# A hybrid decoder layer: the 16 meta tokens worked in tiles of 128 partitions, with the high and low halves of their operands in one matmul

## The chip, the cores and the metric

One core of one Trainium2 chip runs the whole layer as one program. The metric is device microseconds of one execution; a measurement is the median of several runs. "Full clock" below is TensorE's granted clock of 2.4 GHz, "half clock" 1.2 GHz.

## The reference

The layer puts 16 learned meta tokens ahead of 1024 tokens of width 1024, normalises the stream and projects it once. Two mixers share the projection: retention with 4 heads of 128, worked in chunks of 128 tokens of which the meta tokens are a partial first one, and sparse attention with 8 heads of 64, where an indexer picks the top 256 keys of each query. Output projection and a squared-ReLU MLP follow, and the meta tokens are dropped.

```python
h = jnp.concatenate([meta, x], axis=1)
u = rmsnorm(h, norm1_w[l]).astype(h.dtype)
proj = u @ w_in[l]
...
y_ret = retention(rq, rk, rv, rg, ret_norm_w[l], pos)
y_dsa = sparse_attention(dq, dk, dv, iq, ik, iw, q_norm_w[l], k_norm_w[l], rel_bias, pos, topk)
h = h + jnp.concatenate([y_ret, y_dsa], axis=-1) @ w_out[l]
u = rmsnorm(h, norm2_w[l])
h = h + jnp.square(jax.nn.relu(u @ w_ff1[l])) @ w_ff2[l]
return h[:, N_META:]
```

## The kernel before, in words

Matmuls run in a reduced-precision form of float32 (fp32r). To keep accuracy, an operand is split into a high half (a ScalarE copy to fp32r) and a low half (what is left, a VectorE or GpSimd subtract), and a product becomes three matmuls: high by high, low by high, high by low. Tokens are worked in eight blocks of 128; the meta tokens are a ninth block, b == 8, of 16 partitions.

`proj` (L225 to L231) projects one block: for each of 8 slices of the width, three matmuls with the block's inputs as weights (128 or, for the meta block, 16 columns) and a slice of the weight matrix streaming past. `umh` and `uml` hold the meta block's inputs. `small_proj` (L254) gives the index key, attention key and value of a block; for values, `vv[:, b]` holds the high half in 64 columns and the low half in the next 64. `ret_meta` (L427) starts a retention head: it projects the meta tokens to keys and values, rotates the keys, and multiplies them by the values over 16 rows (L435) to the state `S`.

The program has these stages: normalisation and index scores (to about 190 us), retention of 4 heads by 8 chunks together with the top-k search on VectorE and ScalarE (to about 436 us), attention together with the output projection (to about 645 us), second normalisation, MLP. Attention goes by units, (block i, half of the heads g), i from 0 to 7. `attend_p` makes the scores and exponentials of a unit; `attend_v` (L571) multiplies its probabilities by the values. For each tile of keys, the meta tile first and then i + 1 tiles of 128, it transposes the probabilities of four heads on TensorE (L581), splits them (L587 on ScalarE, L588 on VectorE) into `ph` and `pl`, and adds `vv` by `ph` (L589) and `vv` by `pl` (L590) in PSUM. For the meta tile these have 16 rows.

Memory comes from pools. `p1` (called `big`) holds the working tiles of the index and retention stages and is closed by `stage.close()` (L768); then `p2` opens over the same memory, and the first writer of each of its tiles waits for the last readers of `p1`. The last of those is the store of a retention head's output (`oh`, scaled on VectorE in L485) to DRAM (L486). Python code is recorded in the order written; a list scheduler then orders each engine's instructions by its own estimate, and every engine executes its list strictly in that order. Waits between engines are semaphores.

Of the kernel before, what the change touches and what calls it, by code (L numbers as in the profile page):

```python
# [9 lines left out]
F32 = mybir.dt.float32  # L10
F32R = mybir.dt.float32r
# [9 lines left out]
NM = 16  # L21
NB = 8
# [58 lines left out]
def layer(ctx, tc, x, meta, norm1_w, w_in, ret_w, q_w, k_w, rel, w_out, norm2_w, w1, w2,  # L81
# [91 lines left out]
    umh = const.tile([128, 8, NM], F32R, name="umh")  # L173
    uml = const.tile([128, 8, NM], F32R, name="uml")

# [42 lines left out]
    def u_sl(b, d):  # L218
        if b == 8:
            return umh[:, d, :], uml[:, d, :]  # L220
        o = 128 * (b % 4)
        return uth[b // 4][d // 4][:, d % 4, o:o + 128], utl[b // 4][d // 4][:, d % 4, o:o + 128]

    def proj(ps, b, hs, ls, c0, n):
        P = NM if b == 8 else 128  # L225
# [7 lines left out]
    def do_norm1(b):  # L233
        if b == 8:
            xm = row("xt")
            nc.sync.dma_start(xm[:NM, :D], meta)
            norm_T(xm[:NM, :D], NM, lambda g: (umh[:, 4 * g:4 * g + 4, :], uml[:, 4 * g:4 * g + 4, :]))
# [9 lines left out]
    absw = const.tile([128, NB, 8], F32, name="absw")  # L247
    sgnw = const.tile([128, NB, 8], F32, name="sgnw")
    w8 = const.tile([128, NB, 8], F32, name="w8")
# [3 lines left out]
    def small_proj(b, hs, ls):  # L253
        P = NM if b == 8 else 128  # L254
        ps = psA()
        proj(ps, b, hs, ls, 0, NS)
        s = big.tile([128, NS], F32, name="smp", tag="fg", bufs=2)
        nc.scalar.activation(s[:P], ps[:P, :NS], AF.Copy)
# [4 lines left out]
        nc.vector.tensor_tensor(vv[:P, b, 64:128], s[:P, 136:200], vv[:P, b, 0:64].bitcast(F32), op=ALU.subtract)  # L263
        if b < 8:
# [120 lines left out]
    kgain = const.tile([128, 64], F32, name="kgain")  # L385
    nc.sync.dma_start(kgain, bcast(k_w, 64))
    qgain = const.tile([128, 64], F32, name="qgain")
# [26 lines left out]
    def rotate(ps, P, b, nqk, name):  # L414
# [5 lines left out]
        ro = big.tile([128, 2, 2, 64], F32, name="ro", tag="ro", bufs=2)  # L420
        nc.gpsimd.tensor_tensor(ro[:P, :nqk, 0], t1[:P, :nqk, 0], t2[:P, :nqk, 1], op=ALU.subtract)
# [5 lines left out]
    def ret_meta(h):  # L427
        hs, ls = st["w", h]
        ps = psA()
# [141 lines left out]
    def attend_v(i, g):  # L571
# [6 lines left out]
        for k, (b, k0, kp) in enumerate(tiles):  # L578
# [568 lines left out]
```

## Time and profile before

| | us |
|---|---|
| median of 3 runs | 1327.14 (1326.75 to 1327.76) |
| the profiled execution's own time | 1329.52 |
| its span, first to last instruction | 1327.7 |
| TensorE busy | 1271.8 (96%) |
| VectorE busy | 1076.9 (81%) |
| ScalarE busy | 750.4 (57%) |
| GpSimd busy | 260.8 (20%) |

PE is TensorE, PEld its weight loads, DVE VectorE, ACT ScalarE, POOL GpSimd, SP the engine that issues the transfers. Matmuls are pipelined, so the printed duration of one is longer than the time after which the next one starts. A matmul's form is printed as rows*columns of its weights, then the columns that stream past: 16*128 16x512 has 16 rows in use, 128 columns of weights and streams 512. A line number is that of the kernel before.

### The profile page before, as it was taken

The page shows a single profiled execution, that of the slowest core. Times are in us where ns is not written, and L with a number is a line of the kernel's source. Part 1 is how long each engine was busy: PE and PEld are TensorE (multiplying, and loading weights), DVE is VectorE, ACT ScalarE, POOL GpSimd, SP SyncE. Part 2 cuts the span into 40 slices and gives each one's busy share as a digit, 9 for nine tenths or more (in the row PEclk, how much of TensorE's full clock was granted, in tenths as well). Part 3 has the DMA queues.
Part 4 walks back from the last instruction along what each step waited for, and adds up shares of the span by engine and source line. Part 5 has one row for each costly group of instructions (what it writes and reads, how often), then busy time and mean ns, then how long its engine had stood idle before and what let it go on. Part 6 is the DMA issues. An engine that isn't in the chain of part 4 may idle for free. (4 is left out here: it accounts for less than half of the span.)

```text
span 1327.7 us, 18666 instructions
## 1 busy us (share of the span) xinstructions
PE 1271.8 (96%) x6200; PEld 1047.9 (79%) x6200; DVE 1076.9 (81%) x2387; ACT 750.4 (57%) x1593; POOL 260.8 (20%) x297
## 2 busy tenths in 40 slices
PE   6999999899899999999997999999999999999998
PEld 5888868687777778787775888888888888888887
DVE  5678999899979878676759877777878988887875
ACT  6676647577753667565756555555556444444442
POOL 4004472323434424220343000000000200000000
PEclk9999999899999899999998999999999999999999
DMA  9103040202201211212362434434538844434222
GB/s 283 57 17 90 33 133 9 72 11 71 64 16 49 95 64 49 67 45 72 112 213 88 156 130 161 148 129 173 175 135 298 334 160 159 158 134 184 96 95 96
DMA packets 93664, 153.74 MB, mean 116 GB/s; under 512 B 7240, under 2 KB 47344, under 8 KB 89856
## 3 DMA queue, kind: packets, MB, share of 16 engines
q1 hardware_dynamic: 93568, 152.56, 33.5%
q8 instruction: 49, 0.80, 0.2%
q14 instruction: 47, 0.39, 0.1%
HBM read 110.58 MB, written 43.46 MB: 116 GB/s over the span
## 5 line engine op out<-in xcount | busy, mean ns | idle before, releaser
L898 ACT ACTIVATE wh<-ga 128x512 fp32r<-128x512 f32 x144 | 87.2, 628 | 158.7 <-PE psB L1046 141.5
L229 PE MATMUL psA<-wh,uh 128*128 128x512 f32 x376 | 152.4, 406 | 4.4 <-DVE gs L455 4.3
L231 PE MATMUL psA<-wl,uh 128*128 128x512 f32 x376 | 150.4, 400 | 0.0
L230 PE MATMUL psA<-wh,ul 128*128 128x512 f32 x376 | 150.1, 399 | 0.0
L899 DVE TENSOR_TENSOR wl<-ga,wh 128x512 fp32r<-128x512 f32 x144 | 96.7, 687 | 47.4 <-ACT wh L898 46.8
L898 ACT ACTIVATE wh<-sum 128x512 fp32r<-128x512 f32 x128 | 78.6, 625 | 74.3 <-DVE sum L895 69.9
L1046 PE MATMUL psB<-wh,wl 128*128 128x512 f32 x280 | 108.9, 389 | 0.0
L1047 PE MATMUL psB<-wl,wh 128*128 128x512 f32 x280 | 108.9, 389 | 0.0
L1045 PE MATMUL psB<-wh 128*128 128x512 f32 x280 | 106.8, 389 | 0.0
L689 DVE TENSOR_SCALAR_CACHE_REDUCE jk_cnt<-sc,tcand 128x400 bf16<-128x400 f32 (+1 forms) x124 | 102.2, 824 | 1.0
L694 ACT ACTIVATE jk_top<-sc,tcand 128x272 bf16<-128x272 f32 (+2 forms) x93 | 85.0, 914 | 28.2 <-DVE tcand L728 23.6
L899 DVE TENSOR_TENSOR wl<-sum,wh 128x512 fp32r<-128x512 f32 x128 | 87.7, 685 | 6.4 <-ACT wh L898 4.7
L229 PEld LDWEIGHTS psA<-wh,uh 128*128 128x128 f32 x376 | 72.2, 192 | 19.0 <-issue 3.5
L191 POOL TENSOR_TENSOR wl<-wr,wh 128x512 fp32r<-128x512 f32 x56 | 80.9, 1460 | 31.2 <-PE psB L641 15.5
L965 POOL COPY ga<-wl 128x1 f32<-128x1 f32 x8 | 6.6, 826 | 401.6 <-PE psB L928 276.2
L231 PEld LDWEIGHTS psA<-wl,uh 128*128 128x128 f32 x376 | 71.9, 191 | 14.4
L230 PEld LDWEIGHTS psA<-wh,ul 128*128 128x128 f32 x376 | 72.4, 192 | 13.5
L587 ACT ACTIVATE ph<-psB 128x512 fp32r<-128x512 f32 (+1 forms) x88 | 51.3, 592 | 48.3 <-PE psB L581 40.3
L588 DVE TENSOR_TENSOR ph<-psB,ph 128x512 fp32r<-128x512 f32 (+1 forms) x88 | 59.4, 683 | 17.4 <-ACT ph L587 15.9
L335 ACT ACTIVATE rl<-psB,absw 128x320 f32<-128x320 f32 (+5 forms) x104 | 52.7, 554 | 36.4 <-PE psB L333 23.9
L1046 PE MATMUL psA<-wh,wl 128*128 128x512 f32 x168 | 65.4, 389 | 0.0
L1047 PE MATMUL psA<-wl,wh 128*128 128x512 f32 x168 | 65.4, 389 | 0.0
(354 smaller groups left out, 3669.9 us busy)
## 6 DMA issues: line engine op xcount, KB each, us to landing
ga<-hid SPq DMA_DIRECT2D x28, 1024.0 KB, 4.9
wr<-in_w_ff_dram SPq DMA_DIRECT2D x34, 512.0 KB, 4.8
hid<-hs SPq DMA_DIRECT2D x48, 256.0 KB, 2.0
wr<-in_w_in_dram SPq DMA_DIRECT2D x32, 256.0 KB, 3.2
gb<-in_w_ff_dram SPq DMA_DIRECT2D x8, 1024.0 KB, 4.9
ga<-in_w_ff_dram SPq DMA_DIRECT2D x8, 1024.0 KB, 5.6
wr<-in_w_out_dram SPq DMA_DIRECT2D x12, 512.0 KB, 3.8
xt<-in_x_dram SPq DMA_DIRECT2D x8, 512.0 KB, 4.6
```

What stands on the lines that cost most here:

```text
L191: (nc.vector if alt and altc[0] % 2 else nc.gpsimd).tensor_tensor(shl, raw, shp.bitcast(F32), op=ALU.subtract)
L229: nc.tensor.matmul(ps[:P, :n], uh, wh, start=d == 0, stop=False)
L230: nc.tensor.matmul(ps[:P, :n], ul, wh, start=False, stop=False)
L231: nc.tensor.matmul(ps[:P, :n], uh, wl, start=False, stop=d == 7)
L588: nc.vector.tensor_tensor(pl[:kp], tp[:kp], ph[:kp].bitcast(F32), op=ALU.subtract)
L689: nc.vector.tensor_scalar(jk_[:, :ncol[i]], sc[i], cand[:, j:j + 1], 0.0, op0=ALU.is_ge, op1=ALU.add, accum_out=cnt[:, j:j + 1])
L694: nc.scalar.activation(jk_top[:, :ncol[i]], sc[i], AF.Sign, scale=-1.0, bias=cand[:, j:j + 1], accum_out=cnt[:, j:j + 1])
L898: nc.scalar.activation(view(hi), s, AF.Copy)
L899: nc.vector.tensor_tensor(view(lo), s, view(hi).bitcast(F32), op=SUB)
L1045: nc.tensor.matmul(ps[tb], ah[:, t], bh, start=j == 0 and m not in CONT, stop=False, skip_group_check=True)
L1046: nc.tensor.matmul(ps[tb], al[:, t], bh, start=False, stop=False, skip_group_check=True)
L1047: nc.tensor.matmul(ps[tb], ah[:, t], bl, start=False, stop=j == NO - 1, skip_group_check=True)
```

## The change

Three things are done to the meta block. First, `um` replaces `umh` and `uml`: 48 columns of weights per slice, the high half in columns 0 to 15, zeros, the low half in 32 to 47. `proj_meta` streams the high half of the weight matrix past all 48 and its low half past the first 16, so 16 matmuls replace 24; the two results stand in different partitions of PSUM and are added (a ScalarE copy, then a VectorE add), for the small projection and for the four retention heads. Second, `vv[:, 8]` is zeroed and holds the values twice, in partitions 0 to 15 and 32 to 47, and a new tile `pm`, zeroed once, takes the high half of the meta probabilities in its first 16 partitions and the low half from partition 32 on: one matmul over 128 rows replaces two over 16. Third, the rotated key and the value tile of `ret_meta` are zeroed by GpSimd and multiplied over 128 rows. To make room, some small tables move between pools.

```diff
-    umh = const.tile([128, 8, NM], F32R, name="umh")
-    uml = const.tile([128, 8, NM], F32R, name="uml")
+    um = const.tile([128, 8, ML + NM], F32R, name="um")
+    nc.vector.memset(um.bitcast(F32), 0.0)
...
+    def proj_meta(hs, ls, c0, n, tag, bufs):
+
+        ps = psA()
+        for d in range(8):
+            if d:
+                nc.tensor.matmul(ps[:NM, :n], um[:, d - 1, :NM], ls[d - 1][:, c0:c0 + n], start=False, stop=False)
+            if d == 7:
+                nc.tensor.matmul(ps[:NM, :n], um[:, d, :NM], ls[d][:, c0:c0 + n], start=False, stop=False)
+            nc.tensor.matmul(ps[:ML + NM, :n], um[:, d, :], hs[d][:, c0:c0 + n], start=d == 0, stop=d == 7)
+        t, s = [big.tile([128, 256], F32, name="mt", tag=tag, bufs=bufs) for _ in range(2)]
+        nc.scalar.activation(t[:NM, :n], ps[ML:ML + NM, :n], AF.Copy)
+        nc.vector.tensor_tensor(s[:NM, :n], ps[:NM, :n], t[:NM, :n], op=ALU.add)
+        return s
...
+    nc.vector.memset(vv[:, 8].bitcast(F32), 0.0)
...
+        if b == 8:
+            s = proj_meta(hs, ls, 0, NS, "oh", 3)
...
+        if b == 8:
+            nc.scalar.activation(vv[ML:ML + NM, b], vv[:NM, b].bitcast(F32), AF.Copy)
...
+        if P < 128:
+            nc.gpsimd.memset(ro[:, :nqk], 0.0)
...
-        ps = psA()
-        proj(ps, 8, hs, ls, 128, 256)
-        km = rotate(ps, NM, 8, 1, "km")
+        kv = proj_meta(hs, ls, 128, 256, "qkT", 2)
+        km = rotate(kv, NM, 8, 1, "km")
         vm = big.tile([128, 128], F32, name="vm", tag="vz", bufs=2)
-        nc.scalar.activation(vm[:NM], ps[:NM, 128:256], AF.Copy, scale=vecs[:NM, 2, h:h + 1])
+        nc.gpsimd.memset(vm, 0.0)
+        nc.scalar.activation(vm[:NM], kv[:NM, 128:256], AF.Copy, scale=vecs[:NM, 2, h:h + 1])
         pd = psB()
-        nc.tensor.matmul(pd[:, 0:128], km[:NM, 0], vm[:NM], start=True, stop=True)
+        nc.tensor.matmul(pd[:, 0:128], km[:, 0], vm, start=True, stop=True)
...
+            if b == 8:
+                ph, pl = at["pm"], at["pm"][ML:]
             nc.scalar.activation(ph[:kp], tp[:kp], AF.Copy)
             nc.vector.tensor_tensor(pl[:kp], tp[:kp], ph[:kp].bitcast(F32), op=ALU.subtract)
-            nc.tensor.matmul(pv, vv[:kp, b, :], ph[:kp], start=k == 0, stop=False)
-            nc.tensor.matmul(pv, vv[:kp, b, :], pl[:kp], start=False, stop=k == len(tiles) - 1)
+            nc.tensor.matmul(pv, vv[:, b, :], ph, start=k == 0, stop=False)
+            if b < 8:
+                nc.tensor.matmul(pv, vv[:, b, :], pl, start=False, stop=k == len(tiles) - 1)
...
     stage.close()
     p2["p"] = ctx.enter_context(tc.tile_pool(name="p2", bufs=1))
+    at["pm"] = p2["p"].tile([128, 512], F32R, name="pm")
+    nc.vector.memset(at["pm"].bitcast(F32), 0.0)
```

The new line numbers are shifted: L485 becomes L506, L556 L577, L562 L583, L581 L602, L588 L611, L589 L612, L554 and L555 L575 and L576, L594 L618. The order of instructions moves in many places; two matter below. VectorE at the change of pools, before (the waits are named by the semaphore's engine; DMAHW are the transfers'):

```order
L556 ISA P,mn<-psA,mb 128x240 [waits PE_49]
L556 ISA mn 128x1
L485 SCALAR_TENSOR_TENSOR oh<-oh,rs_y,fg 128x128 [waits Pool_49]
L485 SCALAR_TENSOR_TENSOR oh<-oh,rs_y,fg 128x128 x3
L562 TENSOR_REDUCE m_5222<-mn 128x1 [waits DVE_49,Activation_49]
L562 TENSOR_REDUCE m_5245<-mn 128x1 [waits DVE_49,Activation_49]
L588 TENSOR_TENSOR ph<-psB,ph 128x512 [waits Activation_49]
```

The same place now:

```order
L506 SCALAR_TENSOR_TENSOR oh<-oh,rs_y,fg 128x128 [waits Pool_49]
L506 SCALAR_TENSOR_TENSOR oh<-oh,rs_y,fg 128x128 x3
L795 MEMSET pm 128x512 [waits DMAHW2_49,DMAHW7_49,DMAHW0_49,DVE_49]
L611 TENSOR_TENSOR pm<-psB,pm 16x512 [waits Activation_49] x2
L577 ISA P,mn<-psA,sc 128x32
L577 ISA mn 128x1
L577 ISA P,mn<-psA,mb 128x240
```

The fill of `pm` stands directly behind the scaling of `oh`, with waits on transfers that include the store of that `oh`, and both meta subtracts of block 0 stand behind it. Before, those waits stood in this list at the first probabilities of block 2:

```order
L556 ISA P,mn<-psA,mb 128x240 [waits PE_49]
L556 ISA mn 128x1
L601 TENSOR_TENSOR ytmp<-psB,ytmp 64x256 [waits Activation_49]
L562 TENSOR_REDUCE m_5287<-mn 128x1 [waits DVE_49]
L556 ISA P,mn<-psA,sc 128x160 [waits DMAHW2_49,DMAHW7_49,DMAHW0_49,PE_49]
```

TensorE at the same time, before, from the matmul of the second meta tile on:

```order
L589 MATMUL psB<-ph,vv 128x512
L581 MATMUL psB<-ident,P 128x128 x8
L554 MATMUL psA<-knh,qs 128x32
L555 MATMUL psA<-knl,qs 128x32
L590 MATMUL psB<-ph,vv 128x512
L594 MATMUL psB<-ident,rs 128x128 x4
```

And now:

```order
L575 MATMUL psA<-knh,qs 128x32
L576 MATMUL psA<-knl,qs 128x32
L612 MATMUL psB<-pm,vv 128x512
L602 MATMUL psB<-ident,P 16x128 x4
L612 MATMUL psB<-pm,vv 128x512
L602 MATMUL psB<-ident,P 128x128 x8
L618 MATMUL psB<-ident,rs 128x128 x4
```

Both meta matmuls of block 0 and the four small transposes between them (the second head half's meta tile) now stand directly ahead of the eight full transposes; before, each meta tile had two matmuls, spread among the scores of block 1.

## Rows read from the trace of the kernel before

**Rows 1.** Busy time by stage; after the stretch: its length, five engines, clock, transfers.

```profile
core 0: us, PE busy (x) PEld busy (x) DVE busy (x) ACT busy (x) POOL busy (x), PEclk, DMA share, GB/s
40.00:190.00 150.00, 146.96 (x793) 124.49 (x792) 127.40 (x268) 96.79 (x215) 53.50 (x50) 1.00 0.20 62
190.00:391.00 201.00, 188.21 (x941) 154.65 (x941) 185.44 (x602) 137.05 (x364) 67.97 (x102) 0.97 0.15 44
...
436.00:452.00 16.00, 15.56 (x73) 12.04 (x70) 10.68 (x50) 9.20 (x29) 6.11 (x6) 0.68 0.23 80
452.00:645.00 193.00, 186.44 (x1061) 149.44 (x1062) 145.60 (x467) 123.33 (x247) 47.44 (x32) 1.00 0.19 61
```

**Rows 2.** TensorE in order of time (start, duration, ...): a plain run in retention.

```profile
252.13 0.39 PE L229 MATMUL psA<-wh,uh 128*128 128x512 f32 x1
...
253.94 0.39 PE L231 MATMUL psA<-wl,uh 128*128 128x512 f32 x1
```

**Rows 3.** TensorE in order of time around a meta tile in attention.

```profile
509.88 0.40 PE L590 MATMUL psB<-ph,vv 128*128 128x512 f32 x1
510.12 0.60 PE L527 MATMUL psA<-ident,qr 128*128 128x128 f32 x4
...
510.68 0.28 PE L555 MATMUL psA<-knl,qs 128*128 128x256 f32 x1
510.88 0.50 PE L589 MATMUL psB<-ph,vv 16*128 16x512 f32 x1
511.31 0.66 PE L581 MATMUL psB<-ident,P 128*128 128x128 f32 x4
```

**Rows 4.** TensorE in order of time: head 0's projection of the meta tokens.

```profile
170.39 0.39 PE L231 MATMUL psA<-wl,uh 128*128 128x512 f32 x1
170.62 0.28 PE L229 MATMUL psA<-wh,umh 128*16 128x256 f32 x1
...
171.20 0.28 PE L231 MATMUL psA<-wl,umh 128*16 128x256 f32 x1
171.32 0.31 PE L332 MATMUL psB<-ikh,iq 128*128 128x320 f32 x1
```

**Rows 5.** TensorE in order of time: L435, and a full-height product of its size.

```profile
192.09 0.39 PE L231 MATMUL psA<-wl,uh 128*128 128x512 f32 x1
192.41 0.48 PE L435 MATMUL psB<-vm,ro 16*128 16x128 f32 x2
192.82 0.50 PE L229 MATMUL psA<-wh,uh 128*128 128x512 f32 x1
...
237.09 0.39 PE L468 MATMUL psB<-qkT 128*128 128x128 f32 x2
237.31 0.39 PE L470 MATMUL psB<-vz,ro 128*128 128x128 f32 x2
```

**Rows 6.** All engines in order of time, 436 to 446 us; last the store's landing.

```profile
437.43 0.59 ACT L587 ACTIVATE ph<-psB 16x512 fp32r<-16x512 f32 x1
438.68 0.29 ACT L481 ACTIVATE jk<-oh 128x128 bf16<-128x128 f32 x1
439.42 1.03 POOL L141 TENSOR_TENSOR rs_y<-rs_y,nhalf 128x4 f32<-128x4 f32 x1
441.12 0.67 DVE L588 TENSOR_TENSOR ph<-psB,ph 16x512 fp32r<-16x512 f32 x1
442.14 1.97 PE L581 MATMUL psB<-ident,P 128*128 128x128 f32 x8
442.15 1.42 DVE L485 SCALAR_TENSOR_TENSOR oh<-oh,rs_y,fg 128x128 f32<-128x128 f32 x4
...
yrd<-oh SPq DMA_DIRECT2D x1, 256.0 KB, 2.2
```

**Rows 7.** Waits of VectorE, 190 to 400 us: total, times, longest.

```profile
DVE t L418 <- PE psA L231: 4.2, 5, 2.4
```

**Rows 8.** Groups by line (busy us, mean ns | idle before): nearest to added work.

```profile
L601 DVE TENSOR_TENSOR ytmp<-psB,ytmp 64x256 f32<-64x256 f32 x32 | 13.4, 417 | 4.2 <-ACT ytmp L600 3.7
...
L375 POOL MEMSET sc<- 128x144 f32 x1 | 0.2, 218 | 0.0
```

More of the change, by code (lines that the diff above doesn't have):

```diff
@@ L21 @@
 NM = 16
+ML = 32
 NB = 8
@@ L218, in u_sl @@
     def u_sl(b, d):
-        if b == 8:
-            return umh[:, d, :], uml[:, d, :]
         o = 128 * (b % 4)
         return uth[b // 4][d // 4][:, d % 4, o:o + 128], utl[b // 4][d // 4][:, d % 4, o:o + 128]
+    def proj_meta(hs, ls, c0, n, tag, bufs):
[10 more added lines that the diff above has]
+        return s
     def proj(ps, b, hs, ls, c0, n):
-        P = NM if b == 8 else 128
+        P = 128
         for d in range(8):
@@ L236, in do_norm1 @@
             nc.sync.dma_start(xm[:NM, :D], meta)
-            norm_T(xm[:NM, :D], NM, lambda g: (umh[:, 4 * g:4 * g + 4, :], uml[:, 4 * g:4 * g + 4, :]))
+            norm_T(xm[:NM, :D], NM, lambda g: (um[:, 4 * g:4 * g + 4, :NM], um[:, 4 * g:4 * g + 4, ML:]))
         else:
@@ L246, in layer @@
     vv = kp_.tile([128, 9, 128], F32R, name="vv")
-    absw = const.tile([128, NB, 8], F32, name="absw")
-    sgnw = const.tile([128, NB, 8], F32, name="sgnw")
-    w8 = const.tile([128, NB, 8], F32, name="w8")
+    nc.vector.memset(vv[:, 8].bitcast(F32), 0.0)
+    absw = px.tile([128, NB, 8], F32, name="absw")
+    sgnw = px.tile([128, NB, 8], F32, name="sgnw")
+    w8 = px.tile([128, NB, 8], F32, name="w8")
     kss = const.tile([128, 9], F32, name="kss")
@@ L254, in small_proj @@
         P = NM if b == 8 else 128
-        ps = psA()
-        proj(ps, b, hs, ls, 0, NS)
-        s = big.tile([128, NS], F32, name="smp", tag="fg", bufs=2)
-        nc.scalar.activation(s[:P], ps[:P, :NS], AF.Copy)
+        if b == 8:
+            s = proj_meta(hs, ls, 0, NS, "oh", 3)
+        else:
+            ps = psA()
+            proj(ps, b, hs, ls, 0, NS)
+            s = big.tile([128, NS], F32, name="smp", tag="fg", bufs=2)
+            nc.scalar.activation(s, ps[:, :NS], AF.Copy)
         jk64 = jk[:, :64]
@@ L384, in layer @@
     vecs = pk[:, 1664:1676].rearrange("p (k h) -> p k h", k=3)
-    kgain = const.tile([128, 64], F32, name="kgain")
+    kgain = big.tile([128, 64], F32, name="kgain")
     nc.sync.dma_start(kgain, bcast(k_w, 64))
-    qgain = const.tile([128, 64], F32, name="qgain")
+    qgain = big.tile([128, 64], F32, name="qgain")
     nc.sync.dma_start(qgain, bcast(q_w, 64))
@@ L428, in ret_meta @@
         hs, ls = st["w", h]
-        ps = psA()
-        proj(ps, 8, hs, ls, 128, 256)
-        km = rotate(ps, NM, 8, 1, "km")
+        kv = proj_meta(hs, ls, 128, 256, "qkT", 2)
+        km = rotate(kv, NM, 8, 1, "km")
         vm = big.tile([128, 128], F32, name="vm", tag="vz", bufs=2)
-        nc.scalar.activation(vm[:NM], ps[:NM, 128:256], AF.Copy, scale=vecs[:NM, 2, h:h + 1])
+        nc.gpsimd.memset(vm, 0.0)
+        nc.scalar.activation(vm[:NM], kv[:NM, 128:256], AF.Copy, scale=vecs[:NM, 2, h:h + 1])
         pd = psB()
-        nc.tensor.matmul(pd[:, 0:128], km[:NM, 0], vm[:NM], start=True, stop=True)
+        nc.tensor.matmul(pd[:, 0:128], km[:, 0], vm, start=True, stop=True)
         S = big.tile([128, 128], F32, name="S", tag="S", bufs=2)
```

## The prediction

> **What bounds the kernel now.** I read three views in this order: the busy time by stage, the instructions in order of time around each meta-token step, and the waits and groups of VectorE; beside them the built order of the changed program.
>
> The stage table [rows 1] shows TensorE nearly full in every stage the change touches. In the index stage it is busy for 147 of 150 us, in the attention stage (452 to 645 us) for 186 of 193. The retention stage is different: VectorE is busy for 185 of 201 us and TensorE for 188 of 201, so each waits for the other. Between 436 and 452 us, where the last retention head and the first attention units overlap, TensorE looks full, but its granted clock is 0.68: about ten of the sixteen microseconds at the 1.2 GHz level, the rest at 2.4. So TensorE time removed there should come off the end, while in the retention stage it need not.
>
> A plain run gives the yardstick: nine full-height 512-column matmuls start within 1.81 us, first to last [rows 2], 0.23 us each. I count start to start, since the printed durations (0.39) overlap.
>
> **The change, part by part.**
>
> *Probabilities of the meta tile (L589, L590 before).* An attention unit issues two 16-row matmuls of 512 columns. Around one [rows 3] the trace shows a 256-column neighbour starting 0.20 us before it, where 256 columns take 0.12 [rows 4], and the next instruction starting 0.43 us after it, where 512 full-height columns take 0.23. That is 0.08 + 0.20 = 0.28 us beyond its columns; the other instructions of this kind that run at the full clock and wait for nothing look alike (32 in all). The new form is one matmul of 128 rows, so both gaps and one matmul go: 2 x 0.28 + 0.23 = 0.79 us per unit. For the 14 units from block 1 on this is **-11.1 us**. Beside it ScalarE and VectorE do what they did (one 16x512 copy, one subtract), so nothing else becomes late, except that the one matmul now waits for the subtract as well; if every unit paid half of the subtract's 0.67 us [rows 6], 14 x 0.34 = 4.7 us would come back. I take none of it, because other matmuls stand between in the built order, and keep it for the range. [...]
>
> *Meta projections.* A projection loses 8 of 24 matmuls. A retention one (256 columns) steps by 0.116 us (five steps in 0.58) [rows 4]: 0.9 us per head. The small one (200 columns) then steps by 0.09: **-0.7 us**, in a part of the program where TensorE is the bound. The 16-row product of keys and values (L435) costs 0.32 + 0.41 us from the start of the instruction ahead to the one behind [rows 5]; less 0.23 for the one ahead that is 0.50. A full-height pair of the same size takes 0.22 (237.09 to 237.31) [rows 5]: 0.28 per head. Head 0 has its projection inside the index stage, TensorE-bound: **-1.2 us** for both. Heads 1 to 3 have theirs where VectorE is nearly full; of VectorE's idle time there only 4.2 us is for a projection [rows 7]. I count their 3.6 us as zero. What is added stands on VectorE: an add of 16x256 from PSUM, nearest row the 64x256 one at 0.42 us [rows 8], three times **+1.3 us**. Bounds for these heads: -3.6 (TensorE decides after all, the add is covered) to +2.5 (each add also waits 0.4 us for ScalarE's copy, taken like the add).
>
> *Added and hidden.* The zero fills of um and vv run while VectorE waits for the first transfers. Those of ro and vm are on GpSimd, busy for 68 of 201 us [rows 1], which does not hold TensorE up here; uncovered, eight at 0.2 us (its 128x144 fill took 218 ns [rows 8]) would be 1.6 us. The moved small tables change no work.
>
> *The new buffer pm.* It lies in the memory of the first pool, and its zero fill has to wait for the last reader of that pool: the store of the last head's output (L486 before). In the built order VectorE fills pm right behind the scaling that feeds this store; before, the first VectorE instruction with that wait came 19 rows later, when the store had landed. ScalarE's first copy into pm waits behind it, and so do both meta matmuls of block 0. With the old durations [rows 6]: ScalarE's square 438.68, GpSimd done at 440.45, four scalings 1.42, so 441.9; store to landing 2.2, so 444.1; fill, between nothing and the 0.67 of a 512-column subtract, say 0.4; copy 0.59; subtract 0.67, so 445.8. Then the first matmul and four transposes (at half clock 0.43 and 1.0), and, as there is one pm, copy and subtract once more: 448.5. Behind that stand the eight transposes that started at 442.14 before: +6.4 us. The program has by then one 16-row matmul less to come (0.7 at half clock), so I take **+6.0 us**. Bounds: 0, if TensorE finds other work, and +9, if the emptied TensorE stays at the 1.2 GHz level for as long again (6 us of work at half clock cost 3).
>
> *Sum:* -11.1 - 0.7 - 1.2 + 1.3 + 6.0 = **-5.7 us**. The profiled execution took 1329.5 us (span 1327.7), 2.4 above the median of the runs, 1327.1; the change is small, so I take it off the median: **1321.4 us**.
>
> **The rivals.**
>
> *A, the store's wait is covered.* For it: scaling could come earlier, as there is less ahead of it, and in the old stretch VectorE was idle for a third of the time [rows 1]. Against it: three queues in order stand behind one landing. Without the +6.0 the time is 1315.4, and with the retention heads' 3.6 us as well instead of +1.3, 1310.5.
>
> *B, the gaps belong to the step and not to its height.* If the matmul behind a small transpose and a subtract always opens 0.28 us, only the columns go: the units give 14 x (0.28 + 0.23) = 7.1 if one gap stays per unit, and 3.2 if both stay; 1325.4 to 1329.3. Against it: the full-height matmul of the tile before, with the same subtract and a transpose around it, is followed after 0.24 us (509.88 to 510.12) [rows 3].
>
> *C, slower: widths alternate.* The new projections alternate weights of 48 and 16 columns, 16 switches each, 80 in all. If each opened the 0.28 us of a height switch, 22.4 us would be added: 1343.8. At 0.07 us a switch the gain is gone, at 0.11 the kernel is slower by 0.2%. The rows speak against it: from 128 to 16 columns and back the steps are as long as the columns alone [rows 4]; a 48-column one they do not show. [...]
>
> *D, slower: the switch of pools runs long.* If VectorE's stop empties TensorE for over 14 us in all, the gain is gone; the price of 6 would have to more than double. About 1331.
>
> **How the numbers follow.** Forecast (1317 to 1326) 0.55, A 0.24, B 0.09, C 0.06, D 0.06. About 0.2%, 2.7 us, is what a measurement of this kernel can tell from no change. Below 1324.5 lie A and most of the forecast: faster 0.71. The top of the forecast, most of B and a little of D make the same: 0.20. Slower: 0.09. The range takes in the bounds of the forecast and most of A and B: 1311 to 1328.
>
> **What would show it.** In the attention stage every pm matmul should be followed after 0.23 us, and the stage from the first unit of block 1 to its end should be about 11 us shorter. At the pool switch TensorE should be idle for some 4 to 6 us before the first pm matmul, with the fill of pm as what it leads back to, beginning when the store lands. Projections of the meta tokens should step by 0.12 us in both widths. I am wrong if the steps at pm stay above 0.3, if the widths open gaps, if the fill does not wait, or if the retention stage moves by more than 4 us.

## The result, and the profile after

The changed kernel takes **1339.77 us** (1337.21 to 1340.34, 4 runs) against 1327.45 for the kernel before in the same session: a ratio of 1.0084, interval 1.0062 to 1.0106. It is slower by 12 us where 6 us less were forecast, and it lies outside the range. The profiled execution took 1337.21 us (span 1335.4), 7.7 above the one of before. The views below are of that one, so they account for 7.7 us and not for all 12.

Busy time by stage of the changed kernel; after the stretch stand its length, the five engines, the clock, the transfers' share and GB/s:

```profile
40.00:190.00 150.00, 147.45 (x796) 125.94 (x795) 125.60 (x262) 95.97 (x214) 47.98 (x49) 0.99 0.19 59
190.00:391.00 201.00, 186.40 (x931) 154.75 (x931) 189.03 (x616) 141.41 (x373) 72.36 (x109) 0.96 0.17 49
...
436.00:460.00 24.00, 13.58 (x75) 10.93 (x75) 15.81 (x63) 10.74 (x31) 7.04 (x6) 0.72 0.18 58
460.00:652.00 192.00, 180.47 (x1035) 148.05 (x1036) 145.73 (x461) 120.60 (x243) 46.53 (x31) 0.99 0.18 60
```

Against [rows 1] two things differ. At the change of pools TensorE is busy for 13.6 of 24 us. In the attention stage it is busy for 6 us less, and the stage is no shorter: from the first meta matmul of block 1 to the first one of the last unit it takes 187.8 us before (451.52 to 639.36) and 188.4 now (458.27 to 646.66). TensorE's waits from 436 to 660 us say what it does instead (total us, times, longest):

```profile
PE psB L612 <- DVE pm L611: 11.4, 10, 7.0
PE psA L575 <- DVE mn L577: 4.1, 10, 0.7
PE psA L548 <- DMA qr<-qd: 3.4, 1, 3.4
```

The first row is `pm`'s matmul waiting for VectorE's subtract into it. 8.4 of the 11.4 us fall at the change of pools. The second row is TensorE waiting until VectorE has read scores out of PSUM; before, it was this:

```profile
PE psA L554 <- DVE mn L556: 1.2, 2, 0.8
```

TensorE at the change of pools, in order of time (start, duration; in brackets idle time and what ended it):

```profile
439.24 0.38 PE L576 MATMUL psA<-knl,qs 128*128 128x32 f32 x1
446.64 0.77 PE L612 MATMUL psB<-pm,vv 128*128 128x512 f32 x1 [7.03 <-DVE pm L611]
447.21 1.05 PE L602 MATMUL psB<-ident,P 128*16 128x128 f32 x4
449.65 0.80 PE L612 MATMUL psB<-pm,vv 128*128 128x512 f32 x1 [1.39 <-DVE pm L611]
450.25 1.91 PE L602 MATMUL psB<-ident,P 128*128 128x128 f32 x8
```

VectorE in the same stretch, which answers to [rows 6]:

```profile
439.13 3.06 DVE L506 SCALAR_TENSOR_TENSOR oh<-oh,rs_y,fg 128x128 f32<-128x128 f32 x4
444.60 0.48 DVE L795 MEMSET pm<- 128x512 f32 x1 [2.41 <-issue]
445.86 0.68 DVE L611 TENSOR_TENSOR pm<-psB,pm 16x512 fp32r<-16x512 f32 x1 [0.78 <-ACT pm L610]
448.92 0.68 DVE L611 TENSOR_TENSOR pm<-psB,pm 16x512 fp32r<-16x512 f32 x1 [2.38 <-ACT pm L610]
```

That is the forecast chain, link by link: scalings, 2.41 us of idle time until the store has landed (issued at 442.21 us, 2.2 us to landing as before; `issue` says that the profile names nothing that ended this wait), the fill, ScalarE's copy, the subtract, the matmul, then copy and subtract once more. Only the stop is longer, 7.0 us where 4 to 6 were expected, and a second one of 1.4 us follows.

A meta tile later in the attention stage, which answers to [rows 3] (the copy and the subtract, then TensorE's weight load and matmul, with what they wait for):

```profile
527.46 0.57 ACT L610 ACTIVATE pm<-psB 16x512 fp32r<-16x512 f32 x1
529.23 0.68 DVE L611 TENSOR_TENSOR pm<-psB,pm 16x512 fp32r<-16x512 f32 x1
...
529.47 0.27 PE L576 MATMUL psA<-knl,qs 128*128 128x240 f32 x1
529.96 0.19 PEld L612 LDWEIGHTS psB<-pm,vv 128*128 128x128 f32 x1 [0.41 <-DVE pm L611]
529.96 0.50 PE L612 MATMUL psB<-pm,vv 128*128 128x512 f32 x1 [0.22 <-DVE pm L611]
530.30 0.40 PE L664 MATMUL psB<-wh,ys 128*128 128x512 f32 x1
```

The subtract comes up 1.2 us after the copy has ended, behind other work in VectorE's order. The 240 columns ahead take 0.11 us and the step is 0.49; the step behind is 0.34 and not 0.23. The gap ahead has a new owner: it was the 16 rows, it is the subtract.

A further loss stands at the start, where no step of the prediction looked. TensorE there:

```profile
19.98 0.67 PE L156 MATMUL psB<-ident,u 16*128 16x16 f32 x8
24.73 1.94 PE L156 MATMUL psB<-ident,u 128*128 128x128 f32 x8 [4.08 <-DVE u L151]
26.46 0.42 PE L301 MATMUL psB<-ident,smp 128*64 128x128 f32 x1
26.53 0.51 PE L231 MATMUL psA<-wsh,um 128*48 128x200 f32 x1
```

The scheduler now puts the eight transposes of block 2's normalised input ahead of block 1's small projection, and TensorE waits 4.1 us for the normalisation. Before, that projection's 24 matmuls ran from 22.1 to 25.9 us, beside the normalisation:

```profile
22.11 0.28 PE L229 MATMUL psA<-wsh,uh 128*128 128x200 f32 x1
...
25.94 0.41 PE L231 MATMUL psA<-wsl,uh 128*128 128x200 f32 x1
...
27.60 1.03 PE L155 MATMUL psB<-ident,u 128*128 128x128 f32 x8
```

The first index scores come 3.0 us later than before. The last chunk of retention comes 1.2 us earlier all the same, since the retention stage is 4.8 us shorter. In the profiled executions the 7.7 us therefore lie behind it; each stretch runs up to the instruction named:

| stretch, up to | us before | us now | TensorE idle before | now |
|---|---|---|---|---|
| the first index scores | 44.7 | 47.7 | 10.9 | 14.1 |
| the last index scores | 137.7 | 138.2 | 2.8 | 2.4 |
| retention's last product with `sm` | 254.3 | 249.5 | 17.1 | 19.4 |
| the first meta matmul of block 1 | 14.9 | 22.8 | 0.4 | 10.3 |
| the first matmul of the MLP | 246.3 | 247.5 | 11.1 | 16.1 |
| the end | 629.9 | 629.7 | 13.6 | 12.7 |

TensorE's busy time falls by 11.4 us in all (1271.8 to 1260.4), and its idle time rises by 19.1. The work did go; new waits cost more than it gave.

### The profile page after: what moved, and what is told of

Its sections match the earlier page's. It is cut to its first block, busy times and chain, and to the rows that moved or that the text cites. A ratio compares the mean times of both kernels' runs of the same rounds, so it can differ in the third digit from the quotient of the medians.

```text
span 1335.4 us, 18540 instructions
## 1 busy us (share of the span) xinstructions
PE 1260.4 (94%) x6144; PEld 1044.1 (78%) x6144; DVE 1080.1 (81%) x2395; ACT 752.5 (56%) x1598; POOL 264.7 (20%) x305
## 5 line engine op out<-in xcount | busy, mean ns | idle before, releaser
L192 POOL TENSOR_TENSOR wl<-wr,wh 128x512 fp32r<-128x512 f32 x56 | 78.2, 1413 | 20.3 <-ACT wh L189 13.2
L611 DVE TENSOR_TENSOR ph<-psB,ph 128x512 fp32r<-128x512 f32 x72 | 49.2, 687 | 20.4 <-ACT ph L610 15.6
L1071 PE MATMUL psA<-wh 128*128 128x512 f32 x168 | 64.9, 389 | 0.0
```

The source lines that it names most:

```text
L192: (nc.vector if alt and altc[0] % 2 else nc.gpsimd).tensor_tensor(shl, raw, shp.bitcast(F32), op=ALU.subtract)
L1071: nc.tensor.matmul(ps[tb], ah[:, t], bh, start=j == 0 and m not in CONT, stop=False, skip_group_check=True)
```

## The experiments

Seventeen kernels ran. "The attention stretch" is the time from retention's last product with `sm` to the first matmul of the MLP, in the profiled execution: 261.2 us before, 270.3 after. The kernel before took 1326.8, 1325.8, 1326.6, 1325.8 and 1325.6 us in the five sessions; one kernel's single runs lie some 10 us apart, so medians are compared and ratios, to the kernel before in the same session, carry their intervals. A ratio is not the quotient of the medians and differs from it by up to 0.25%.

### Which part costs

**pm_only** adds to the kernel before the attention part alone (the small tables move, to make room).

```diff
+    nc.vector.memset(vv[:, 8].bitcast(F32), 0.0)
...
+            if b == 8:
+                ph, pl = at["pm"], at["pm"][ML:]
...
+    at["pm"] = p2["p"].tile([128, 512], F32R, name="pm")
+    nc.vector.memset(at["pm"].bitcast(F32), 0.0)
```

> The kernel before with the attention part of the change alone (pm, the doubled meta rows of vv, one matmul), and the small tables moved to make room. Theory 1, the pool switch and lateness: the wait for the last store costs 7 to 8 us as in the changed kernel, and what the attention stage saves after it (10 to 13 us) is given back there by work that comes late in this particular order; then 1333 to 1336 us. Rival 2, the attention stage saves its 11 us and what ate them came from the other parts of the change: about 1324. Rival 3, the built order alone moves the time by several us whatever is edited: no figure, but the start (to 190 us) then differs from that of the kernel before by more than 1 us, though nothing there was edited but two small fills.

Measured: 1336.55 us, 1.0067 (1.0044 to 1.0090). As theory 1 had it: the attention part alone makes most of the loss, and the attention stretch takes 267.0 us. Rival 3's sign is there as well (the first index scores come 2.2 us earlier), which `tables` below answers.

**meta_only** is the change without its attention part.

```diff
-    at["pm"] = p2["p"].tile([128, 512], F32R, name="pm")
-    nc.vector.memset(at["pm"].bitcast(F32), 0.0)
...
-                ph, pl = at["pm"], at["pm"][ML:]
```

> The changed kernel with its attention part undone (two 16-row matmuls per unit, no pm, no switch of pools ahead of its time); the projections of the meta tokens and the full-height product of keys and values stay. Theory 1: the start loses 3.6 us to the order of block 2's transposes, the retention stage wins 4.7 back, the rest is as before: 1325 to 1328. Rival 2 (the other parts of the change are what costs): over 1330. My own sum for these parts alone was -0.6: 1326.8, for another reason (no loss at the start).

Measured: 1330.0 us, 1.0018 (0.9996 to 1.0041). The first index scores come 2.2 us late, the attention stretch is that of before (261.4). The time lies between theory 1 and rival 2 and could be no change; this part is settled further down.

**late_pm** sets `pm` up at block 2; blocks 0 and 1 keep two 16-row matmuls.

```diff
-    at["pm"] = p2["p"].tile([128, 512], F32R, name="pm")
-    nc.vector.memset(at["pm"].bitcast(F32), 0.0)
...
+        if u == 5:
+            at["pm"] = p2["p"].tile([128, 512], F32R, name="pm")
+            nc.vector.memset(at["pm"].bitcast(F32), 0.0)
```

> The changed kernel, but the units of blocks 0 and 1 keep two 16-row matmuls and pm is set up only at block 2, when the last store of the pool before has long landed. Theory 1: TensorE's stop of 7 us at the switch is gone, two of the 14 units lose their 0.8 us: about 1333 if the attention stage goes on giving back what it saves, 1324 if its losses followed from the stop. Rival (the stop costs nothing in the end, since TensorE is not what binds there): 1339 as in the changed kernel.

Measured: 1328.65 us, 1.0004 (0.9983 to 1.0025), 11 us below the changed kernel and between the two figures of theory 1. So the stop at the change of pools decides whether the kernel is slower. But with the stop gone there is still no gain: the attention stretch is 260.8 us, as in meta_only, though 12 units have one matmul where that has two.

**tables** moves the small tables and nothing else.

```diff
-    absw = const.tile([128, NB, 8], F32, name="absw")
+    absw = px.tile([128, NB, 8], F32, name="absw")
```

> The kernel before with nothing but the three small tables and two gains moved to other memory: no instruction added or taken away. Theory 1: 1327, within 1.5. Rival 3, that any edit reorders the program and this alone moves the time as much as the change did: off by more than 4 us either way.

Measured: 1328.13 us, 0.9998 (0.9973 to 1.0024). The order moves (the first index scores come 1.9 us earlier, some scores of the attention stage up to 10.7 us earlier) and the time doesn't. A reordering of this size is not what costs 12 us.

### Where the attention stage's gain goes

**early_pm** puts `pm` into the attention's own memory, so that it waits for no pool.

```diff
+    PM = ap_.tile([128, 512], F32R, name="pm")
+    nc.gpsimd.memset(PM.bitcast(F32), 0.0)
...
-        th = big.tile([128, 128], F32, name="th", tag="th", bufs=2)
+        th = big.tile([128, 128], F32, name="th", tag="th", bufs=1)
```

> The changed kernel with pm in the attention's own memory, set to zero early in the retention stage; room comes from one buffer of th instead of two and a shorter table. All 16 units use one matmul. Theory 1 (the stop at the switch of pools is worth about 10 us, the rest stays given back in the attention stage): like late_pm (1328.7) less 1.6 for the two units more: 1327. Rival 2 (the stop isn't the cause, late_pm was luck of the order): 1334 or more. Rival 4 (one buffer of th costs in the retention stage): the last sm is over 2 us later than in late_pm.

Measured: 1336.38 us, 1.0082 (1.0056 to 1.0109): theory 1 is off by 9 us. TensorE in order of time there:

```profile
441.05 0.50 PE L614 MATMUL psB<-pm,vv 128*128 128x512 f32 x1 [0.32 <-DVE pm L613]
...
446.04 0.79 PE L614 MATMUL psB<-pm,vv 128*128 128x512 f32 x1 [3.71 <-DVE pm L613]
```

And VectorE:

```profile
442.20 3.08 DVE L508 SCALAR_TENSOR_TENSOR oh<-oh,rs_y,fg 128x128 f32<-128x128 f32 x4 [0.33 <-POOL rs_y L142]
...
445.31 0.68 DVE L613 TENSOR_TENSOR pm<-psB,pm 16x512 fp32r<-16x512 f32 x1
```

The store is out of it and TensorE still stops for 3.7 us, since the subtract into `pm` stands in VectorE's order behind the four scalings. What hurts is the wait for the subtract; the pool only made it longer. (This kernel's last chunk of retention is also 3.9 us later than late_pm's, with one buffer of `th`; rival 4 may account for that much.)

**late_defer** is late_pm with `pm`'s matmul written behind the two matmuls of the next tile.

```diff
+            if b < 8 or not new:
+                nc.tensor.matmul(pv, vv[:kp, b, :], ph[:kp], start=k == new, stop=False)
+                nc.tensor.matmul(pv, vv[:kp, b, :], pl[:kp], start=False, stop=k == len(tiles) - 1 and (k > 1 or not new))
+            if k == 1 and new:
+                nc.tensor.matmul(pv, vv[:, 8, :], at["pm"], start=False, stop=len(tiles) == 2)
```

> late_pm, with the matmul of pm written behind the two matmuls of the next tile of its unit, so that VectorE's subtract into pm has long ended when it comes up. Theory 5 (the single matmul waits for the subtract in nearly every unit: 11 steps ahead of a pm matmul were 4.5 us too long in late_pm): 1324, and the step ahead of pm at its columns' time. Rival 6 (TensorE waits for something else then: VectorE's scores, a late load, the clock): 1328 again, with the excess moved to other steps.

Measured: 1319.36 us, 0.9942 (0.9920 to 0.9965): 9.3 us less than late_pm, 6.5 less than the kernel before. The attention stretch falls from 260.8 to 251.1 us. Theory 5 predicted 4.5; the matmul's own wait carries only half of it.

**no_meta_mm** leaves the meta tile's matmuls out of the kernel before.

```diff
+            if b == 8:
+                yield
+                continue
```

> The kernel before without the two matmuls of the meta tile in the attention units (their share is missing from the output; transposes, copy and subtract stay). It is what the attention part can bring at most. If TensorE is the bound throughout, 16 x (2 x 0.28 + 2 x 0.23) = 16.3 us: 1311. If, as late_pm suggests, TensorE runs into VectorE or late loads when it is relieved, half of it or less: 1319 to 1325.

Measured: 1313.35 us, 0.9900 (0.9872 to 0.9928): 12.5 us, short of 16.3 and above half of it. TensorE does bind here, for the larger part.

**after_defer** is the changed kernel with the deferral alone; `pm` still waits for the store. In this and in early_defer block 0's two units, which take turns in the one `pm`, both read the second one's probabilities; the work is the same, but the second copy no longer waits for the first matmul, so a part of the gain (the second stop was 1.4 us) may be that.

> The changed kernel as it is (pm in the second pool, set to zero behind the store), with the matmul of pm written behind the two matmuls of the next tile. Theory 7 (what costs is that one matmul has to wait for VectorE: for the scalings and the fill at the switch, for the subtract in every unit; the wait of the fill for the store hurts only through it): TensorE's stop of 7 us shrinks under 2, the attention stage gains its 10: 1320 to 1323. Rival 8 (the fill waiting for the store stops VectorE and ScalarE whatever TensorE does): the stop stays at 4 us or more: 1328 or more.

Measured: 1323.45 us, 0.9974 (0.9948 to 1.0000): 16 us below the changed kernel. The fill still waits for the store (it starts at 444.23 us) and TensorE's waits for `pm` from 430 to 460 us come to 0.3 us in all; the longest wait there is now 2.0 us for scores. Rival 8 falls: the fill's wait hurt because a matmul waited behind it.

**early_defer**, the same for early_pm.

> early_pm with the same deferral. There pm is free of the store, and TensorE still stopped for 3.7 us, since the subtract into pm stood behind the four scalings on VectorE. Theory 7: that stop goes, as do the 12 steps of 0.6 us too much ahead of pm: 1336.4 - 3.7 - 7.7 = 1325, or like late_defer (1319.4) if early_pm's other loss (its last sm was 3.9 us later than in late_pm) came from the order as well. Rival: over 1330.

Measured: 1315.72 us, 0.9909 (0.9877 to 0.9940): 20.7 us below early_pm, more than the steps add up to. The attention stretch falls from 264.9 to 243.5 us; early_pm has 17 us of this stretch at half clock and early_defer 3.4, which is worth up to 7 of these 21 us. Half clock is a granted clock of 0.50: at it, 512-column matmuls of the kernel before start every 0.427 us (six steps from 245.12 to 247.68 us), which is 1.2 columns per ns; at 1.00 they start every 0.227 us.

**before_defer** defers the two 16-row matmuls of the kernel before, in blocks 1 to 7.

```diff
+            late = i > 0
+            if b < 8 or not late:
...
+            if k == 1 and late:
+                nc.tensor.matmul(pv, vv[:NM, 8, :], qh[:NM], start=False, stop=False)
+                nc.tensor.matmul(pv, vv[:NM, 8, :], ql[:NM], start=False, stop=False)
```

> The kernel before, its two 16-row matmuls kept, only written behind the two matmuls of the next tile (blocks 1 to 7). Theory 9 (deferral helps by itself: the old second matmul waited for the subtract too): 1321 to 1324. Theory 7 alone (only the single matmul has to wait; the old first one needed ScalarE's copy and the second stood 0.6 us behind it): 1326 to 1328, no change.

Measured: 1317.3 us, 0.9939 (0.9911 to 0.9967). Theory 7 alone is wrong on this point: the old form profits as well. TensorE in order of time shows one reason:

```profile
515.20 0.39 PE L594 MATMUL psB<-ph,vv 128*128 128x512 f32 x1
515.52 0.49 PE L596 MATMUL psB<-ph,vv 16*128 16x512 f32 x1
515.86 0.39 PE L597 MATMUL psB<-ph,vv 16*128 16x512 f32 x1
516.18 0.66 PE L581 MATMUL psB<-ident,P 128*128 128x128 f32 x4
```

Ready together, the two run back to back and cost 0.09 + 0.11 + 0.09 us beyond their columns, where the separate pair of [rows 3] costs 2 x 0.28. A second reason is the clock, which the next part prices.

### Wait, height and count apart

The three kernels of this group share nearly everything but how the meta matmul is issued (two_full has one weight tile more, `vl`). `pm` lies in the memory of `um`, block 0 is as before, the start is repaired.

**um_pm**:

```diff
+            at["pm"] = um_
+            nc.gpsimd.memset(um_.bitcast(F32), 0.0)
```

> The changed kernel with pm in the memory of um, free after head 3's projection and set to zero there by GpSimd, so that no pool is waited for; block 0 keeps its two 16-row matmuls; the start is repaired as in late_start_fix; pm's matmul directly behind its subtract, as in the change. If the wait for the subtract gives back the attention stage's gain: like late_start_fix, 1325 to 1327. If the gain was lost through pm's place in memory and the late blocks: 1318 or less.

Measured: 1325.25 us, 0.9971 (0.9948 to 0.9994).

**um_pm_defer** adds the deferral of late_defer, for blocks 1 to 7.

> The same with the matmul of pm behind the two matmuls of the next tile (blocks 1 to 7). If the wait for the subtract is the cause: 8 to 10 us less than um_pm, 1314 to 1317, and the step ahead of pm at its columns' time. If not: within 3 us of um_pm.

Measured: 1316.31 us, 0.9907 (0.9877 to 0.9937): 8.9 us less. The tile view of `um` in um_pm (durations in ns min/median/max, then start times; below, who waited, us and times):

```profile
L620 PE MATMUL psB<-um,vv x14: 393/498/506, 448.4 to 632.4; 128*128 128x512 f32 x14
...
  PEld psB L620: 6.9, 13
  PE psB L620: 3.4, 11
```

And in um_pm_defer:

```profile
L623 PE MATMUL psB<-um,vv x14: 387/394/402, 453.4 to 634.3; 128*128 128x512 f32 x14
...
  DVE um L618: 1.6, 4
```

In um_pm the weight load of `vv` is held in 13 of 14 units and the matmul in 11; it then takes 0.50 us where a prepared one takes 0.39. Deferred, neither TensorE nor its weight loads wait for `um`.

**two_full** issues two matmuls of 128 rows on the same `pm`, one per half; `vl` holds the values in partitions 32 to 47 and zeros elsewhere.

```diff
+                nc.tensor.matmul(pv, vv[:, 8, :], at["pm"], start=False, stop=False)
+                nc.tensor.matmul(pv, vl, at["pm"], start=False, stop=False)
```

> um_pm_defer with two matmuls of 128 rows on pm, one against the weights of the upper halves and one against those of the lower (zeros elsewhere), instead of one against both: the count of the kernel before, the height of the change. If the second matmul costs its columns and no more, 14 x 0.23 = 3.2 us more than um_pm_defer. If heights cost nothing in pairs, it is no faster than before_defer (1317.3) by more than the start's 1 us; if 16 rows cost 0.35 us a unit even in pairs, as the steps in before_defer read, it is 4 to 5 us below it, less what the start differs.

Measured: 1318.36 us, 0.9947 (0.9926 to 0.9969): 2.05 us above um_pm_defer, of the size of 14 matmuls by 0.23, and the intervals overlap. Of height the median tells nothing, since it lies 1 us above before_defer. Two things stand between these: the projections part, which before_defer hasn't, and the clock at the change of pools. All engines from 436 to 449 us in um_pm_defer (two_full has the same stretch, from 435.8 us):

```profile
436.00:449.00 13.00, 12.91 (x58) 10.56 (x58) 9.38 (x42) 6.95 (x21) 4.31 (x3) 0.61 0.20 65
```

And in before_defer:

```profile
436.00:449.00 13.00, 11.50 (x73) 8.63 (x70) 12.04 (x54) 9.27 (x26) 5.67 (x4) 1.00 0.25 81
```

At 0.61 some 10 of the 13 us lie at half clock, which is worth about 5 us of work; before_defer has none of it. So height is read from the steps. All meta matmuls at full clock, start to start beyond the columns, ahead and behind, mean of each (the step between two neighbours counts for both):

| kernel | meta matmuls | ahead | behind |
|---|---|---|---|
| before | 29 | 0.18 | 0.19 |
| after | 13 | 0.44 | 0.11 |
| um_pm | 15 | 0.40 | 0.11 |
| before_defer | 32 | 0.12 | 0.11 |
| two_full | 30 | 0.03 | 0.02 |
| um_pm_defer | 16 | 0.05 | 0.03 |

The rows of um_pm, two_full and um_pm_defer count one or two 16-row matmuls of block 0 in. The means hold waits: in the kernel before the medians are 0.10 ahead and 0.20 behind, and the longest gap ahead, 1.4 us, holds a wait of 1.2 for ScalarE's copy.

Full height costs next to nothing here (0.05 us a matmul in two_full). The pair of 16 rows costs 0.3 us a unit even when its members are neighbours (0.09 + 0.11 + 0.09 in before_defer). The single matmul behind its subtract costs 0.55 (0.44 + 0.11 in the changed kernel), 1.5 times what one old matmul cost (0.37).

What the clock hides can be estimated from the profiled executions: the span less half of the time for which TensorE is busy at half clock (us), since a step takes about twice as long there (0.43 against 0.23).

| kernel | span | busy at half clock | span less half of that |
|---|---|---|---|
| before | 1327.7 | 40.3 | 1307.5 |
| after | 1335.4 | 44.5 | 1313.1 |
| before_defer | 1314.4 | 26.9 | 1300.9 |
| late_defer_only | 1313.5 | 30.9 | 1298.0 |
| um_pm | 1321.4 | 39.3 | 1301.7 |
| um_pm_defer | 1315.0 | 41.1 | 1294.4 |
| two_full | 1316.7 | 36.9 | 1298.2 |

By this estimate, of one execution each, the deferral gives um_pm 7.3 us and the kernel before 6.6; the other 6.7 of before_defer's 13.3 us are the clock. One matmul in place of the deferred pair gives 2.9 more (late_defer_only, described below, against before_defer), and two_full's second matmul costs 3.8, where 3.2 were expected.

### The other parts

**late_start_fix** is late_pm with block 1's small projection written ahead of block 2's normalisation.

```diff
+        if b == 0:
+            sb1 = small_proj(1, sh, sl)
+            do_norm1(2)
```

> late_pm, with block 1's small projection written ahead of block 2's norm, which puts it back ahead of those transposes on TensorE. Theory 1a: the start wins its 3 to 4 us, and the retention stage, where VectorE and TensorE wait for each other, takes most of them back, as it did the other way round: last sm within 1.5 us of late_pm, time 1328. Rival 1b: the 3 to 4 us come off the end: 1325.

Measured: 1325.12 us, 0.9971 (0.9946 to 0.9997), 3.5 below late_pm. TensorE's idle time ahead of block 2's transposes falls from some 4 us to 0.70, the first index scores come 3.6 us earlier than in late_pm, the last `sm` 2.2. 1b holds in the time, but the session's kernel before was 1 us lower too and the intervals overlap.

**late_defer_fix** joins late_defer and that start.

> late_defer and the repaired start together. If their gains add (9.3 and 3.5 us against late_pm): 1316. If the start is given back further on: 1319.

Measured: 1315.04 us, 0.9912 (0.9879 to 0.9945). In the medians the gains add; the interval overlaps that of late_defer.

**late_defer_only** is the attention part of late_defer on the kernel before, without the projections part.

> The attention part alone on the kernel before: pm from block 2 on, its matmul behind those of the next tile; the projections of the meta tokens as before (so the start of the kernel before, and 16-row products of keys and values). Against late_defer_fix (1315.0), which has the projections part too: if that part is worth what the steps say (0.7 for the small projection, 1.2 for head 0, little in heads 1 to 3), 1317; if its order costs again as in meta_only, 1312 to 1314.

Measured: 1317.38 us, 0.9923 (0.9898 to 0.9949). The projections part, with its start repaired, is worth some 2 us in the medians, and the intervals overlap so far that it could be nothing. Nor does the merge itself show: deferred, the old pair has 0.9939 (before_defer) and the one matmul 0.9923, and these intervals overlap too.

**um_pm_defer_b0** moves one unit of block 0 to `pm` as well.

```diff
-            new = i > 0
+            new = i > 0 or g == 0
```

> um_pm_defer, with the first unit of block 0 on pm and deferred too, so that one of the two waits for VectorE at the switch of pools goes. If the stretch at 1.2 GHz there (10.2 us in um_pm_defer) comes from TensorE's stops at the switch, it shrinks to one window and the time is 1312; if it does not, 1315.5 to 1316.

Measured: 1315.23 us, 0.9921 (0.9892 to 0.9950). The stretch at half clock stays (10.2 us from 433.6). The expectation's window is 3.41 us: in the kernel before and the changed one every stretch at half clock between two at full clock lasts that or two, three or four times that. But TensorE's waits from 425 to 450 us come to 3.1 us here and to 1.7 in um_pm_defer, so the edit didn't take its stops away, and whether the stretch comes from them is not shown. What brings it about is open: late_defer_only, whose block 0 is the old one, has none.

## Why the prediction was wrong

**Attention units, -11.1: the main failure.** The step that failed is the sentence that the one matmul waits for the subtract as well and "I take none of it, because other matmuls stand between in the built order". They do stand there: between the last meta transpose and `pm`'s matmul of the 14 units lie 4 to 14 matmuls with 0.7 to 2.4 us of columns. It is not enough, since copy and subtract take 0.59 + 0.68 us and the subtract comes up behind scores in VectorE's own order. (In um_pm_defer 26 to 55 matmuls lie between.) The step ahead of `pm` was 0.44 us too long on the mean (13 at full clock), so the fall-back of 4.7 us that I kept for the range was the likely case: 0.44 + 0.11 against 2 x 0.37 before, and one matmul of 0.23 less, is 0.42 us per unit and not 0.79, which makes 5.9. The gap of the old matmuls itself was read rightly: 0.30 in the median of the 29 at full clock (not 32), and 0.37 in the mean with its waits, against 0.28.

The other 6 us went to waits that I hadn't priced, 4.1 us for scores to leave PSUM (1.2 before) and one of 3.4 for a late load of queries (`qr`), and to the clock: from block 1 to the MLP TensorE is busy at half clock for 9.5 us, where before it was 3.1. The wait for scores fits the one at `pm`: a matmul that waits holds the scores behind it in TensorE's order, VectorE gets those late, and TensorE then waits for VectorE again. In um_pm_defer against um_pm the steps at `pm` explain 6 of the 8.9 us, and the waits for scores and `qr` from 431 to 684 us fall as well, from 3.7 and 1.6 us to 2.4 and none. For `qr` the link is not shown: its load was issued at 542.80 us, behind a store and a load of `hp` in SyncE's order and about 1 us before TensorE had come to it, and in um_pm_defer it stands ahead of both.

**Pool switch, +6.0: right mechanism, too small.** The chain ran as written; the first meta matmul of block 1 came 6.75 us later than before, out of a retention stage that ended 1.2 earlier, which makes 8. In the medians 11 us hang on it (late_pm). That is near the upper bound of +9, but not for its reason: 0.72 over 24 us is 13 us at half clock, where before had 10 [rows 1], yet TensorE idles in most of it and is busy at half clock for 5.2 us only, where before it was 10.2. Two links were mis-sized. The scalings took 3.06 us instead of 1.42 (last section), and TensorE had nothing left to do from 439.6 us on, a microsecond or two sooner than my stop of 4 to 6 us implies. after_defer shows the deeper miss: the fill and the store were never the cost by themselves, only the one matmul queued behind them.

**Small projection and head 0, -1.9: steps right, result reversed at the start.** The widths open no gap, as forecast; head 0's projection in the changed kernel, which answers to [rows 4]:

```profile
174.18 0.28 PE L231 MATMUL psA<-wh,um 128*48 128x256 f32 x1
174.30 0.28 PE L228 MATMUL psA<-wl,um 128*16 128x256 f32 x1
174.41 0.28 PE L231 MATMUL psA<-wh,um 128*48 128x256 f32 x1
```

Rival C is out. What failed is that I priced the projection where it stood and didn't read the built order of the first 30 us, where 3.0 us by the first index scores, and 3.6 by the last, were lost to block 2's transposes.

**Heads 1 to 3, +1.3: wrong sign in their stage.** From the last index scores to retention's last product the changed kernel takes 4.8 us less than the kernel before, beyond the 4 that I had named as a sign of error. Part of that is a late start taken up. But the six kernels that have the projections part and a repaired start (late_start_fix, late_defer_fix, um_pm, um_pm_defer, two_full, um_pm_defer_b0) take 2.9 to 4.6 us less there too, and five without it (tables, pm_only, before_defer, no_meta_mm, late_defer_only) between 1.3 less and 1.1 more. So the 3.6 us that I counted as zero, because VectorE looked nearly full, come off this stage after all: my lower bound was near the value, and the VectorE adds didn't show. How much of it reaches the end is not shown (late_defer_fix against late_defer_only: some 2 us, within the intervals).

**Rivals.** D came nearest in the time (the switch). It wanted 14 us, though 11.7 would have undone the gain by my own sum, and 8.4 us of stops were enough since the attention term was nil. A is wrong: the store's wait isn't covered. B is half right: in the change as made a gap does stay behind the small transpose and the subtract, and 5.9 us for the units lies between its 3.2 and 7.1. But it is the wait that makes this gap. Written elsewhere, a full-height matmul has next to none (two_full, 0.05 us a matmul), and a pair of 16 rows still has 0.3, which belongs to the height. What no rival said is that a single wait can cost nearly as much as two gaps (0.55 against 0.74 us). My chance for slower, 0.09, was too low, for the price of each term was reckoned alone: two engines in order, with a new wait between them, were treated as a sum.

## What to carry to other kernels

Before merging two matmuls into one, ask what the merged one waits for that the first of the two did not; here each engine ran its list in order, and that wait held what was queued behind it (TensorE stood for 7.0 us at the change of pools, with eight transposes behind it). Write such a matmul behind the next tile's, where accumulation order is free: here that alone was worth 9 us (um_pm_defer against um_pm). The kernel before gained 9 us by it too, of which up to half may be the clock. The order mattered more than the merge. Deferred, the merged form is 10 to 12 us below the kernel before (late_defer_fix 1315.0, um_pm_defer_b0 1315.2) and the old pair 9 (before_defer 1317.3), with overlapping intervals; the change as made is 12 above. And after an edit read the built order at the program's start too: here the scheduler moved block 2's transposes, which the edit doesn't touch, and TensorE waited 4.1 us for their input.

## What the hardware showed unexpectedly

**A VectorE instruction lasted until a GpSimd add beside it had ended.** GpSimd from 437 us in the changed kernel:

```profile
438.04 1.03 POOL L142 TENSOR_TENSOR rs_y<-rs_y,nhalf 128x4 f32<-128x4 f32 x1
439.04 2.21 POOL L562 TENSOR_TENSOR mb<-bias,sc 128x960 f32<-128x960 f32 x1
```

The first of the four scalings (128x128, two inputs from SBUF) began at 439.13 and took 2.27 us, ending 0.15 us after GpSimd's add; the other three took 0.34 each. Before, the scaling [rows 6] began later within the same add and took 0.63 us, again ending 0.15 us after it:

```profile
440.42 2.22 POOL L541 TENSOR_TENSOR mb<-bias,sc 128x960 f32<-128x960 f32 x1
```

In early_pm, after_defer and before_defer the first scaling also ends 0.15 us after that add (in early_pm it took 2.29 us from 442.20, beside an add of 2.20 from 442.14). A subtract that reads one operand from PSUM was not held: the one into `pm` took its usual 0.68 us at 457.53 in the changed kernel, inside such an add (456.69 to 458.92). Against the 0.34 us of the other scalings the price was 1.9 us; what holds the instruction is not shown.

**The matmul whose weight load waited cost more than the wait.** Released by the subtract at 529.96 us in the changed kernel, it took 0.50 us and the next one started after 0.34, where 0.39 and 0.23 are usual. Its weight load (0.19 us) was held too and started with it, where that of the deferred one ran ahead (453.2 against 453.4 us in um_pm_defer).

**The stretch at half clock at the change of pools is no constant.** It lasts about 10 us in the kernel before and in um_pm_defer and is absent in before_defer and late_defer_only, whose times are within 2.5 us of those that have it all the same. It is absent in tables too, at the time of the kernel before.

**Single runs of this kernel differed by the clock.** The 31 runs of the kernel before in the first session took 1321.8 to 1334.3 us at mean granted clocks of 0.991 to 0.978. Less span times (1 - clock), my estimate of what the lower level takes from a TensorE that is always busy, they lie between 1303.5 and 1310.2 us: about half of the scatter goes.
